# Searching the first token block's best keys in the gate stage instead of the query stage

## The chip, the core and the metric

The kernel runs on one core of one Trainium2 chip. The metric is the device time of one execution in microseconds (us); lower is better. The engines are named as the profile names them: PE is TensorE (its weight loads are PEld), DVE is VectorE, ACT is ScalarE, POOL is GpSimd, SP is SyncE, which here issues most of the DMAs. L123 is line 123 of the kernel.

## What is computed

One decoder layer over 512 tokens of width 1024. A token mixer makes a new residual stream; then a retrieval layer picks, per token and per head, 16 of 16384 experts by product keys. The part around the change is the retrieval:

```python
def chunk_fn(hc):
    q = (hc @ w_query).reshape(PEER_CHUNK, PEER_HEADS, PEER_KEY_DIM)
    s1 = jnp.einsum('chk,nk->chn', q[..., :PEER_HALF_DIM], keys_1)
    s2 = jnp.einsum('chk,nk->chn', q[..., PEER_HALF_DIM:], keys_2)
    v1, i1 = lax.top_k(s1, PEER_TOPK_HALF)
    v2, i2 = lax.top_k(s2, PEER_TOPK_HALF)
    cand = (v1[..., :, None] + v2[..., None, :]).reshape(PEER_CHUNK, PEER_HEADS, -1)
    cand_idx = (i1[..., :, None] * N_KEYS + i2[..., None, :]).reshape(PEER_CHUNK, PEER_HEADS, -1)
    top_s, pos = lax.top_k(cand, PEER_TOPK)
    experts = jnp.take_along_axis(cand_idx, pos, axis=-1)
    gate = jax.nn.softmax(top_s.astype(jnp.float32), axis=-1).astype(hc.dtype)
    u = jnp.take(expert_u, experts, axis=0)
    act = jax.nn.gelu(jnp.einsum('chkd,cd->chk', u, hc))
    v = jnp.take(expert_v, experts, axis=0)
    return jnp.einsum('chk,chkd->cd', gate * act, v)
```

There are 8 heads, 128 keys in each half, and 4 blocks of 128 tokens.

## The kernel before

The kernel is one straight program; every engine works off its own instructions in the order in which they are written. Matrices in float32 are used as the sum of two float16 parts. A *unit* is 128 x 1024 weights: `load_unit` (L112) loads it over SP's queue, `high` (L117, ACT) makes the high part, `low` (L123, DVE) the low part, four buffers each; `run_ahead` and `lows_ahead` issue these steps two to four units ahead of their use. `mm3` (L170 to L172) multiplies with three matmuls: high by high, high by low, low by high.

After the token mixer the program has these stages, told here with the names that the prediction uses.

*Query stage* (loop over `ch`, 16 *chunks*, one per head and half of the keys, and a 17th round that finishes the last). PE makes the queries of chunk `ch` for all 512 tokens, then the scores of chunk `ch - 1` against 128 keys (L744, four token blocks side by side), ACT copies them to `sc` (L746), and `top16` on DVE finds the best 16 of 128 for each of the four blocks: MAX8 (the best eight), their indices, a copy of the list with those eight struck out, MAX8 and indices again (L676 to L684). One list is 128 tokens by 128 scores; a *batch* is the lists that go through the five passes together. After chunk 8 `spend(SW)` adds pieces of the next stage's first work, `select(0, t)` for token blocks 1 to 3, from the list `fill`: generators, each `yield` naming an assumed cost in us, drawn until a budget is used up.

*Selection stage.* Token blocks 1 to 3 are selected for a dense way of computing: in each slot PE does four steps of `u_steps` (scores of all experts for these 384 tokens, a unit is eight steps and ends in an activation, L650, to `s_sb`), and DVE takes pieces of the candidates' top 16, of softmax and of decoding indices. It ends with a PE transpose of the indices of block 3 (L883) and ACT copies.

*Gate stage.* For 48 groups of 8 tokens DVE makes four one-hot tensors (`one_hots`, L907 to L910; two buffers each) from the indices and gates, one group ahead, and PE multiplies them (`w_build`, L924 and L925, 16 matmuls a group) into the matrix of gate weights, which ACT copies out (L927) and SP stores to DRAM (`wd`, L929, 1 MB for every two groups). Between the groups PE goes on with `u_steps`, 200 steps over the 48 groups, four or five a group. `spend(owed + WSP)` is called after each group, but `fill` is empty here.

*Main stage.* 128 expert tiles: PE finishes the scores of tile after tile and multiplies them, weighted by the gate matrix, with the values `vn`. Token block 0 goes a sparse way meanwhile: `block0` selects and decodes it on DVE from the lists found in the query stage, then POOL gathers its experts' rows.

The heart of the gate stage's loop, which the change does not alter except for `fill` and `WSP`:

```python
    for g in range(NG):
        nxt = one_hots(g + 1) if g + 1 < NG else None
        n = left[0] // (NG - g)
        left[0] -= n
        u_steps(n)
        w_build(g, hots)
        owed = spend(owed + WSP)
        hots = nxt
```

Of the kernel before, what the change touches and what calls it, by code (L numbers as in the profile page):

```python
# [7 lines left out]
F32 = mybir.dt.float32  # L8
# [8 lines left out]
P = 128  # L17
# [21 lines left out]
GB = 3  # L39
SW = 0.8  # L40
SWE = 15
WSP = 0.25
ADAB = 3
FU = 3
BUD = 3.6
# [19 lines left out]
def body(tc, xt, cols, c_row, ada_n, ada_t, win, pool_w, pup, cvo, wout, wq, keys, ut, un, vn, fg, out, dbg=None):  # L65
    nc = tc.nc
    V, A, G, PE, SP = nc.vector, nc.scalar, nc.gpsimd, nc.tensor, nc.sync
# [3 lines left out]
    dram = es.enter_context(tc.tile_pool(name="dram", bufs=1, space=bass.MemoryType.DRAM))  # L71
# [34 lines left out]

    x1d = dram.tile([T // P, P, D], F32, name="x1d")
    wd = dram.tile([NA // TST, P, P, TST], F32, name="wd")

    def load_unit(src, bufs=4, pool=None):  # L110
        f = (pool or stream).tile([P, 1024], F32, name="unit_f", tag="f32", bufs=bufs)
        SP.dma_start(f, src)  # L112
        return f
# [21 lines left out]
    def run_ahead(n, nl=4, nh=3, ns=2):  # L135
        for j in range(n, min(n + nl, len(units))):
            if j not in loaded:
                loaded[j] = load_unit(units[j])
        for j in range(n, min(n + nh, len(units))):
            if j not in highs:  # L140
                highs[j] = high(loaded[j], WS)
        for j in range(n, min(n + ns, len(units))):
            if j not in halves:
                halves[j] = low(loaded[j], highs[j], WS, eng=G if j in PL else None)

    def next_unit():
        n = used[0]
        used[0] += 1
        run_ahead(n)
        return halves.pop(n)  # L150

    def lows_ahead():
        run_ahead(used[0], nl=0, nh=0, ns=2)


    fill = []

    def spend(us, width=1):
        k = 0
        while us > 0 and fill:  # L160
            g = fill[k % min(width, len(fill))]
            try:
                us -= next(g)
                k += 1
            except StopIteration:
                fill.remove(g)
        return us

    def mm3(o, a, b, start, stop):
        PE.matmul(o, a[0], b[0], start=start, stop=False)  # L170
        PE.matmul(o, a[0], b[1], start=False, stop=False)  # L171
        PE.matmul(o, a[1], b[0], start=False, stop=stop)  # L172
# [343 lines left out]
    for u in range(4):  # L516
        for jj, p in enumerate(half((mxhi, mxlo))):
            j = 2 * u + jj
# [16 lines left out]
    for u in range(4):  # L535
        for jj, p in enumerate(half((ychi, yclo))):
            j = 2 * u + jj
# [81 lines left out]
    def q_tile():  # L619
        return psr.tile([P, 512], F32, name="q_ps", tag="q", bufs=2)  # L620
# [14 lines left out]
    def u_steps(n):  # L635

        while n > 0:
            if not cur:
                cur.update(i=len(S), k=0, w=next_unit(), p=ps_s.tile([P, 512], F32, name="s_ps", tag="s_ps", bufs=2)[:, 0:NA])
            k = cur["k"]  # L640
            hi, lo = cur["w"]
            s = slice(k * P, (k + 1) * P)
            mm3(cur["p"], (hi[:, s], lo[:, s]), (h2hi[:, k, NB:], h2lo[:, k, NB:]), k == 0, k == NDC - 1)
            cur["k"] += 1
            n -= 1
            if cur["k"] == UL:
                lows_ahead()
            if cur["k"] == NDC:
                sg = ring.tile([P, NA], F32, name="s_sb", tag="s_sb", bufs=NS)
                A.activation(sg, cur["p"], AF.Gelu_apprx_tanh, scale=IWS)  # L650
                S[cur["i"]] = sg
                cur.clear()
# [3 lines left out]
    for j in range(TOPK):  # L656
# [4 lines left out]
    vals, idxs = [[[(sel if t else bsel).tile([P, NH, TOPK], dt, name=f"{n}{t}{s}", tag=f"{n}{t}{s}") for s in range(2)]  # L661
                   for t in range(4)] for n, dt in (("v", F32), ("i", U32))]
# [6 lines left out]

    pieces += [(h2_piece, (hf,)) for hf in range(2)]  # L670

    def top16(ch, sc):
        hd, hf = divmod(ch, 2)
        vi = [(vals[t][hf], idxs[t][hf], wqp.tile([P, P], F32, name="s2", bufs=4)) for t in range(4)]
        for t, (v, ix, s2) in enumerate(vi):
            V.max(v[:, hd, 0:8], sc[:, t])  # L676
        for t, (v, ix, s2) in enumerate(vi):
            V.max_index(ix[:, hd, 0:8], v[:, hd, 0:8], sc[:, t])
        for t, (v, ix, s2) in enumerate(vi):
            V.match_replace(s2, v[:, hd, 0:8], sc[:, t], -3.0e38)  # L680
        for t, (v, ix, s2) in enumerate(vi):
            V.max(v[:, hd, 8:16], s2)
        for t, (v, ix, s2) in enumerate(vi):
            V.max_index(ix[:, hd, 8:16], v[:, hd, 8:16], s2)  # L684

    top = sel.tile([P, 4, NH, TOPK], F32, name="top")
    pos = sel.tile([P, 4, NH, TOPK], U32, name="pos")
# [1 line left out]
    def select(h0, t, pool=None, top=top, pos=pos):  # L689

        pool = pool or sel
        v1, v2 = [v[:, h0:h0 + 4] for v in vals[t]]
        cand = pool.tile([P, 4, NCAND], F32, name="cand", bufs=2)

        def add(a0, na, nb, o0):
            o = cand[:, :, o0:o0 + na * nb].rearrange("p h (a b) -> p h a b", b=nb)
            V.tensor_tensor(o, v1[:, :, a0:a0 + na].unsqueeze(3).to_broadcast([P, 4, na, nb]),
                            v2[:, :, None, 0:nb].to_broadcast([P, 4, na, nb]), op=OP.add)

        for a in range(5):  # L700
            add(a, 1, STAIR[a], STARTS[a])
        add(5, 3, 2, STARTS[5])
        add(8, 8, 1, STARTS[8])
        yield 0.8
        hs = range(4)
        s2 = [pool.tile([P, NCAND], F32, name="c2", bufs=8) for h in hs]
        for h in hs:
            V.max(top[:, t, h0 + h, 0:8], cand[:, h])
        yield 0.5
        for h in hs:  # L710
            V.max_index(pos[:, t, h0 + h, 0:8], top[:, t, h0 + h, 0:8], cand[:, h])
        yield 0.5
        for h in hs:
            V.match_replace(s2[h], top[:, t, h0 + h, 0:8], cand[:, h], -3.0e38)
        yield 0.5
        for h in hs:
            V.max(top[:, t, h0 + h, 8:16], s2[h])
        yield 0.5
        for h in hs:
            V.max_index(pos[:, t, h0 + h, 8:16], top[:, t, h0 + h, 8:16], s2[h])  # L720
        yield 0.5

    wqs = ExitStack()
    wqp = wqs.enter_context(tc.tile_pool(name="wqp", bufs=1, reuse_waits="tile"))
    qs = {}
    for ch in range(17):
        if ch < 16:
            if ch < 2:
                p = firsts[ch]
            else:  # L730
                hi, lo = next_unit()
                p = q_tile()
                for k in range(NDC):
                    s = slice(k * P, (k + 1) * P)
                    mm3(p, (hi[:, s], lo[:, s]), (h2hi[:, k], h2lo[:, k]), k == 0, k == NDC - 1)
                lows_ahead()
                if ch == 15:
                    run_ahead(used[0], nl=4, nh=4, ns=4)
            qs[ch] = wqp.tile([P, 512], F32, name="qs", bufs=2)
            A.activation(qs[ch], p, AF.Copy, scale=IWS)  # L740
        if ch:
            p2 = psr.tile([P, 4, P], F32, name="sc_ps", tag="sc", bufs=1)
            for t in range(4):
                PE.matmul(p2[:, t], qs[ch - 1][:, t * P:(t + 1) * P], keyt[:, (ch - 1) % 2], start=True, stop=True)  # L744
            sc = wqp.tile([P, 4, P], F32, name="sc", bufs=3)
            A.activation(sc, p2, AF.Copy)  # L746
            if ch == 16:
                u_steps(NDC)
                run_ahead(used[0], nl=4, nh=4, ns=4)
            top16(ch - 1, sc)  # L750
        if ch == 8:
            for t in range(1, 4):
                fill.append(select(0, t))
        if ch < SWE:
            spend(SW)
        if pieces:
            f, a = pieces.pop(0)
            f(*a)
# [185 lines left out]
    while fill or late:  # L944
        u_steps(4)
        slot += 1
        while late and late[0][2] + LAG <= slot:
            f, a, _ = late.pop(0)
# [3 lines left out]
    ss_.close()  # L952
    ws_ = ExitStack()
    wpool = ws_.enter_context(tc.tile_pool(name="wpool", bufs=1, side="right", reuse_waits="tile"))
    NG = NA // TG
    hots = one_hots(0)
    owed = 0.0
    left = [max(0, (NS - HOLD - len(S)) * NDC)]
# [5 lines that stand above are left out]
        w_build(g, hots)  # L964
        owed = spend(owed + WSP)
        hots = nxt
    assert not fill
    u_steps((NS - len(S)) * NDC - cur.get("k", 0))
    ws_.close()
    rs.close()  # L970
# [244 lines left out]
```

## Time and profile before

| what | us |
|---|---|
| runs, median of 3 | 1474.02 (1470.59 to 1475.1) |
| the profiled execution | 1472.85 |
| its span, first to last instruction | 1471.1 |
| PE busy in the span | 1412.7 |
| DVE busy in the span | 1270.3 |

The profile is of one execution. "Busy" is time in which an engine works on an instruction; matmuls are pipelined, so that the durations of neighbours overlap and the spacing of their starts tells more. In a row of the order of time, brackets at the end say how long the engine sat idle before it and what ended the wait. A row may join several like instructions (x4). In a row of stretches the number after PE, PEld, DVE, ACT and POOL is busy time, then come the granted TensorE clock as a share of full speed, the mean busy share of the DMA engines and GB/s. By the trace the query chunks run from 298 to 400 us, selection to 490, the gate stage to 638.

### The profile page before, as it was taken

What the parts mean: (1) busy time and instruction counts of PE and PEld (TensorE: products, weight loads), DVE (VectorE), ACT (ScalarE), POOL (GpSimd) and SP (SyncE); (2) the same over time, 40 slices, a digit from 0 to 9 for tenths busy, and PEclk for the clock granted to TensorE, in tenths of its full rate; (3) what the DMA queues carried; (4) which work ended last, traced back from release to release, by engine and by line L of the source; (5) the groups of instructions that cost most, each with busy time, mean ns of one, the idle gap of its engine ahead of it and who ended that gap; (6) DMA issues with size and microseconds to landing.
All of it is one profiled execution on the core that took longest, in us unless ns stands there. A gap on an engine that the chain in (4) does not pass through costs nothing.

```text
span 1471.1 us, 21798 instructions
## 1 busy us (share of the span) xinstructions
PE 1412.7 (96%) x7969; PEld 743.1 (51%) x7969; DVE 1270.3 (86%) x2433; ACT 669.9 (46%) x931; POOL 458.3 (31%) x427
## 2 busy tenths in 40 slices
PE   6998999999989999999999999999999999999997
PEld 2443444445545666665555555555555555444443
DVE  6899966479999999958888988888888898899877
ACT  4554374343433788854333333333333333344334
POOL 0576443200000000000454544445445445422212
PEclk9999999999999999999999999999999999999998
DMA  9554533232233477794899999999999999999953
GB/s 386 192 194 172 185 123 137 79 136 87 72 113 129 150 268 269 249 297 174 295 381 364 371 365 361 375 362 358 366 343 377 364 363 342 357 359 337 326 206 134
DMA packets 145278, 386.79 MB, mean 263 GB/s; under 512 B 10897, under 2 KB 60305, under 8 KB 141073
## 3 DMA queue, kind: packets, MB, share of 16 engines
q1 hardware_dynamic: 108304, 251.15, 48.7%
q0 software_dynamic: 36864, 134.23, 24.8%
q8 instruction: 62, 1.02, 0.3%
q14 instruction: 48, 0.39, 0.1%
HBM read 355.98 MB, written 29.36 MB: 262 GB/s over the span
## 4 chain that ended last, share of the span: by engine, by line
PE 52%; DVE 28%; DMA 7%; issue 6%; POOL 4%; ACT 4%; SPq 0%; POOLq 0%; DVEq 0%; ACTq 0%
PE acc L1093 9%; PE acc L1095 9%; PE acc L1092 9%; DVE unit_lo L123 7%; PE s_ps L172 5%; PE s_ps L170 5%; PE s_ps L171 5%; PE mm L179 4%; DMA gat<-vn,eidx 4%; DVE s_ps L327 3%; POOL gat L987 2%; DVE oh L909 2%; DVE o L907 2%; DVE ol L910 2%; DMA unit_f<-ut 1%
## 5 line engine op out<-in xcount | busy, mean ns | idle before, releaser
L123 DVE SCALAR_TENSOR_TENSOR unit_lo<-unit_f,unit_hi 128x1024 f16<-128x1024 f32 x316 | 397.0, 1266 | 83.9 <-ACT unit_hi L117 80.9
L117 ACT ACTIVATE unit_hi<-unit_f 128x1024 f16<-128x1024 f32 x316 | 330.0, 1046 | 52.9 <-DMA unit_f<-ut 40.4
L987 POOL DMA_INDIRECT gat<-un,eidx x128 | 162.5, 1270 | 586.7 <-DVE bgate L826 421.8
L172 PE MATMUL s_ps<-h2hi,unit_lo 128*128 128x384 f16 x1024 | 334.5, 327 | 7.0 <-DVE unit_lo L123 7.0
L170 PE MATMUL s_ps<-h2hi,unit_hi 128*128 128x384 f16 x1024 | 334.6, 327 | 0.0
L171 PE MATMUL s_ps<-h2lo,unit_hi 128*128 128x384 f16 x1024 | 334.5, 327 | 0.0
L1092 PE MATMUL acc<-unit_hi,ghi 128*128 128x512 f16 x768 | 291.1, 379 | 0.6 <-ACT ghi L1042 0.6
L1093 PE MATMUL acc<-unit_lo,ghi 128*128 128x512 f16 x768 | 291.1, 379 | 0.4 <-DVE unit_lo L123 0.4
L1095 PE MATMUL acc<-unit_hi,glo 128*128 128x512 f16 x768 | 229.9, 379 | 0.1
L987 POOL DMA_INDIRECT gat<-vn,eidx x128 | 158.3, 1236 | 212.0 <-DVE bacc L1011 182.0
L1042 ACT ACTIVATE ghi<-g 128x384 f16<-128x384 f32 x128 | 67.0, 523 | 293.0 <-DVE g L1038 226.8
L1011 DVE SCALAR_TENSOR_TENSOR bacc<-gat,bw,bacc 128x1024 f32<-128x1024 f32 x127 | 162.6, 1280 | 14.9 <-DMA gat<-vn,eidx 14.0
L1003 DVE SCALAR_TENSOR_TENSOR gat<-gat,h2b 128x1024 f32<-128x1024 f32 x128 | 154.4, 1221 | 21.2 <-DMA gat<-un,eidx 20.7
L650 ACT ACTIVATE s_sb<-s_ps 128x384 f32<-128x384 f32 x128 | 63.0, 492 | 222.0 <-PE s_ps L172 211.3
L172 PEld LDWEIGHTS <-unit_lo 128*128 128x128 f16 x1176 | 115.5, 98 | 95.5 <-DVE unit_lo L123 9.2
L171 PEld LDWEIGHTS <-unit_hi 128*128 128x128 f16 x1176 | 115.4, 98 | 85.8 <-issue 3.7
L170 PEld LDWEIGHTS <-unit_hi 128*128 128x128 f16 x1176 | 115.7, 98 | 84.6 <-issue 3.2
L1095 PEld LDWEIGHTS <-glo 128*128 128x128 f16 x768 | 75.0, 98 | 91.6 <-DVE glo L1045 1.5
L1092 PEld LDWEIGHTS <-ghi 128*128 128x128 f16 x768 | 75.1, 98 | 88.4 <-ACT ghi L1042 1.6
L1093 PEld LDWEIGHTS <-ghi 128*128 128x128 f16 x768 | 75.1, 98 | 86.2
L179 PEld LDWEIGHTS <-unit_hi 128*128 128x128 f16 x656 | 64.2, 99 | 91.3 <-ACT unit_hi L117 9.1
L371 POOL TENSOR_TENSOR ada_f<-ada_f,crow 128x1024 f32<-128x1024 f32 x32 | 86.0, 2705 | 69.3 <-ACT crow L482 42.9
(229 smaller groups left out, 1689.4 us busy)
## 6 DMA issues: line engine op xcount, KB each, us to landing
unit_f<-ut SPq DMA_DIRECT2D x128, 512.0 KB
unit_f<-vn SPq DMA_DIRECT2D x128, 512.0 KB
wd<-wst SPq DMA_DIRECT2D x24, 1024.0 KB
wr<-wd SPq DMA_DIRECT2D x16, 1536.0 KB
ada_f<-ada_t SPq DMA_DIRECT2D x32, 512.0 KB
unit_f<-win SPq DMA_DIRECT2D x28, 512.0 KB
unit_f<-wq SPq DMA_DIRECT2D x16, 512.0 KB
sig<-ada_n SPq DMA_DIRECT2D x4, 1024.0 KB
```

The lines of the kernel that those rows point to most:

```text
L117: A.activation(hi, f, AF.Copy, scale=scale)
L123: V.scalar_tensor_tensor(lo, f, scale, hi, op0=OP.mult, op1=OP.subtract)
L170: PE.matmul(o, a[0], b[0], start=start, stop=False)
L171: PE.matmul(o, a[0], b[1], start=False, stop=False)
L172: PE.matmul(o, a[1], b[0], start=False, stop=stop)
L179: PE.matmul(p, w[:, s], r[:, k], start=(i == 0 and k == 0), stop=(i == 2 and k == n - 1))
L987: G.indirect_dma_start(out=t, out_offset=None, in_=un if n < HK else vn, in_offset=bass.IndirectOffsetOnAxis(ap=bs["eidx"][:, k:k + 1], ax ...
L1003: V.scalar_tensor_tensor(t, t, 1.0, h2b, op0=OP.mult, op1=OP.mult, accum_out=bs["pre"][:, n:n + 1])
L1011: V.scalar_tensor_tensor(bacc, t, bw[:, k:k + 1], bacc, op0=OP.mult, op1=OP.add)
L1092: PE.matmul(acc[t][h], ghi[:, ts_], vhi[:, h * 512:(h + 1) * 512], start=st, stop=False)
L1093: PE.matmul(acc[t][h], ghi[:, ts_], vlo[:, h * 512:(h + 1) * 512], start=False, stop=False)
L1095: PE.matmul(acc[t][h], glo[:, ts_], vhi[:, h * 512:(h + 1) * 512], start=False, stop=sp)
```

## The change

Block 0's lists are no longer searched in the query stage. Its scores of each chunk, `sc[:, 0]`, are stored to a DRAM tensor `scd` over SP's queue (16 stores of 64 KB), and `top16` there works on the lists of blocks 1 to 3 only. In the gate stage a generator `block0_lists` is put in `fill`: it loads the scores back, four chunks (256 KB) at a time, two loads ahead, and runs the five passes over four lists at a time, with a `yield` after each pass. So there are 4 batches of 5 pieces, each piece four instructions. `WSP`, the budget after a group, is 0.45 instead of 0.25. What might be left over is spent after the loop.

```diff
-WSP = 0.25
+WSP = 0.45
...
+    scd = dram.tile([4, P, 4, P], F32, name="scd")
...
-    def top16(ch, sc):
-        hd, hf = divmod(ch, 2)
-        vi = [(vals[t][hf], idxs[t][hf], wqp.tile([P, P], F32, name="s2", bufs=4)) for t in range(4)]
-        for t, (v, ix, s2) in enumerate(vi):
-            V.max(v[:, hd, 0:8], sc[:, t])
...
+    def top16(lists, pool, bufs):
+
+        vi = [(vals[t][ch % 2][:, ch // 2], idxs[t][ch % 2][:, ch // 2], sc,
+               pool.tile([P, P], F32, name="s2", bufs=bufs)) for t, ch, sc in lists]
+        for v, ix, sc, s2 in vi:
+            V.max(v[:, 0:8], sc)
+        yield 0.9
+        for v, ix, sc, s2 in vi:
+            V.max_index(ix[:, 0:8], v[:, 0:8], sc)
+        yield 1.1
+        for v, ix, sc, s2 in vi:
+            V.match_replace(s2, v[:, 0:8], sc, -3.0e38)
+        yield 1.1
+        for v, ix, sc, s2 in vi:
+            V.max(v[:, 8:16], s2)
+        yield 0.9
+        for v, ix, sc, s2 in vi:
+            V.max_index(ix[:, 8:16], v[:, 8:16], s2)
+        yield 1.1
+
+    def block0_lists(pool):
+        scs = []
+        for c in range(2):
+            scs.append(pool.tile([P, 4, P], F32, name="sc0", bufs=2))
+            SP.dma_start(scs[c], scd[c])
+        for c in range(4):
+            yield from top16([(0, 4 * c + j, scs[c][:, j]) for j in range(4)], pool, 4)
+            if c < 2:
+                scs.append(pool.tile([P, 4, P], F32, name="sc0", bufs=2))
+                SP.dma_start(scs[c + 2], scd[c + 2])
...
-            top16(ch - 1, sc)
+            SP.dma_start(scd[(ch - 1) // 4][:, (ch - 1) % 4], sc[:, 0])
+            for _ in top16([(t, ch - 1, sc[:, t]) for t in range(1, 4)], wqp, 3):
+                pass
...
+    fill.append(block0_lists(wpool))
     NG = NA // TG
...
-    assert not fill
+    spend(1e9)
```

The lines below the new code move by 1 to 21: the low part is L124, the one-hots are L927 to L930, the passes L678 to L690.

DVE at the start of the gate stage, before the change (`o` and `oh`, `ol` are the four one-hots of a group):

```order
L907 TENSOR_TENSOR o_4518<-aT,i_2447 128x1024
L908 TENSOR_TENSOR o_4517<-aT,i_2447 128x1024
L909 TENSOR_TENSOR oh<-o_4518,gT 128x1024
L910 TENSOR_TENSOR ol<-o_4518,gT 128x1024
L907 TENSOR_TENSOR o_4564<-aT,i_2447 128x1024
L908 TENSOR_TENSOR o_4563<-aT,i_2447 128x1024
L909 TENSOR_TENSOR oh<-o_4564,gT 128x1024
L910 TENSOR_TENSOR ol<-o_4564,gT 128x1024
L123 SCALAR_TENSOR_TENSOR unit_lo<-unit_f,unit_hi 128x1024
```

The same place in the changed kernel (`sc_4484` holds the scores of the first four chunks, `v` the values found):

```order
L678 MAX v_2450<-sc_4484 128x8
L678 MAX v_2451<-sc_4484 128x8
L678 MAX v_2450<-sc_4484 128x8
L678 MAX v_2451<-sc_4484 128x8
L927 TENSOR_TENSOR o_4497<-aT,i_2448 128x1024
L928 TENSOR_TENSOR o_4496<-aT,i_2448 128x1024
L929 TENSOR_TENSOR oh<-o_4497,gT 128x1024
L930 TENSOR_TENSOR ol<-o_4497,gT 128x1024
L124 SCALAR_TENSOR_TENSOR unit_lo<-unit_f,unit_hi 128x1024
L927 TENSOR_TENSOR o_4542<-aT,i_2448 128x1024
L928 TENSOR_TENSOR o_4541<-aT,i_2448 128x1024
```

A piece of four stands ahead of the third group's one-hots, and so on, one piece for every two or three groups; the last piece (L690, of the fourth batch) stands ahead of the one-hots of the 45th group.

SP's queue where the gate stage begins, in the changed kernel (`ut` are the units of the expert scores; in brackets the semaphores that an entry waits for):

```order
L113 DMA unit_f<-ut 128x1024 [waits DMAHW7_49,DVE_49]
L697 DMA sc_4484<-scd 128x512 [waits PE_49]
L697 DMA sc_4486<-scd 128x512
L949 DMA wd<-wst 128x2048 [waits Activation_49]
L113 DMA unit_f<-ut 128x1024 [waits DMAHW0_49,DVE_49]
L949 DMA wd<-wst 128x2048 [waits Activation_49]
```

Before, the 24th load of `ut` is followed by the first store of `wd`; now the two first loads of scores stand between them, and the first of them waits for PE.

## Rows read from the trace of the kernel before

**Rows 1.** The page: busy time of the engines, share of the span, instructions.

```profile
PE 1412.7 (96%) x7969; PEld 743.1 (51%) x7969; DVE 1270.3 (86%) x2433; ACT 669.9 (46%) x931; POOL 458.3 (31%) x427
```

**Rows 2.** Stretches: length, busy time of each engine, granted clock, DMA share, GB/s.

```profile
426.00:430.00 4.00, 4.00 (x15) 1.96 (x14) 3.96 (x31) 0.00 (x0) 0.00 (x0) 0.57 0.40 131
430.00:490.00 60.00, 58.24 (x361) 34.50 (x359) 59.45 (x196) 26.88 (x43) 0.00 (x0) 1.00 0.39 123
490.00:600.00 110.00, 107.49 (x1033) 75.33 (x1032) 110.00 (x168) 93.11 (x109) 0.00 (x0) 1.00 0.72 247
600.00:640.00 40.00, 37.86 (x346) 26.33 (x345) 34.34 (x51) 31.88 (x39) 0.00 (x0) 1.00 0.72 244
640.00:1265.00 625.00, 624.60 (x3383) 330.84 (x3382) 537.01 (x785) 237.58 (x327) 276.77 (x217) 1.00 0.95 347
```

**Rows 3.** DVE in order of time, query stage: start, length, instruction, count.

```profile
350.20 0.87 DVE L676 MAX8 v<-sc 128x8 f32<-128x128 f32 x4 [0.17 <-ACT sc L746]
...
354.89 1.20 DVE L123 SCALAR_TENSOR_TENSOR unit_lo<-unit_f,unit_hi 128x1024 f16<-128x1024 f32 x1
...
369.74 0.87 DVE L676 MAX8 v<-sc 128x8 f32<-128x128 f32 x4
...
376.71 0.87 DVE L676 MAX8 v<-sc 128x8 f32<-128x128 f32 x4
```

**Rows 4.** PE in order of time, query and selection stages.

```profile
354.55 1.05 PE L744 MATMUL sc_ps<-keyt,qs 128*128 128x128 f32 x8
...
360.62 1.05 PE L744 MATMUL sc_ps<-keyt,qs 128*128 128x128 f32 x8
...
425.88 0.40 PE L172 MATMUL s_ps<-h2hi,unit_lo 128*128 128x384 f16 x1 [4.89 <-DVE unit_lo L123]
```

**Rows 5.** PE's waits from 290 to 495: total, times, longest.

```profile
PE s_ps L172 <- DVE unit_lo L123: 7.0, 5, 4.9
```

**Rows 6.** DVE in order of time, end of the query stage.

```profile
403.94 3.49 DVE L123 SCALAR_TENSOR_TENSOR unit_lo<-unit_f,unit_hi 128x1024 f16<-128x1024 f32 x3
407.35 0.86 DVE L676 MAX8 v<-sc 128x8 f32<-128x128 f32 x4
...
417.84 0.53 DVE L708 MAX8 top<-cand 128x8 f32<-128x50 f32 x4
```

**Rows 7.** ACT in order of time, end of the query stage.

```profile
392.06 0.60 ACT L746 ACTIVATE sc<-sc_ps 128x512 f32<-128x512 f32 x1 [0.23 <-PE sc_ps L744]
...
404.59 1.05 ACT L117 ACTIVATE unit_hi<-unit_f 128x1024 f16<-128x1024 f32 x1
```

**Rows 8.** DVE in order of time, gate stage.

```profile
489.99 0.68 DVE L907 TENSOR_TENSOR o<-aT,i 128x1024 f16<-128x1024 f16 x1
...
509.13 1.21 DVE L123 SCALAR_TENSOR_TENSOR unit_lo<-unit_f,unit_hi 128x1024 f16<-128x1024 f32 x1
...
515.08 1.21 DVE L123 SCALAR_TENSOR_TENSOR unit_lo<-unit_f,unit_hi 128x1024 f16<-128x1024 f32 x1
...
632.70 0.69 DVE L910 TENSOR_TENSOR ol<-o,gT 128x1024 f16<-128x1024 f16 x1
```

**Rows 9.** ACT's evictions of finished score units, 395 to 500: durations, first and last start.

```profile
L650 ACT ACTIVATE s_sb<-s_ps x21: 471/490/491, 404.2 to 495.5; 128x384 f32<-128x384 f32 x21
```

**Rows 10.** PE in order of time, gate stage.

```profile
515.60 0.22 PE L924 MATMUL w_ps<-o,oh 128*128 128x128 f16 x1
...
516.50 0.33 PE L170 MATMUL s_ps<-h2hi,unit_hi 128*128 128x384 f16 x1
...
518.45 0.22 PE L924 MATMUL w_ps<-o,oh 128*128 128x128 f16 x1
...
637.75 0.22 PE L925 MATMUL w_ps<-o,ol 128*128 128x128 f16 x1
```

**Rows 11.** Waits from 490 to 640: total, times, longest.

```profile
ACT unit_hi L117 <- DMA unit_f<-ut: 17.9, 15, 3.5
PEld L925 <- DVE ol L910: 6.8, 19, 0.5
```

More of the change, by code (lines that the diff above doesn't have):

```diff
@@ L670, in body @@
     pieces += [(h2_piece, (hf,)) for hf in range(2)]
-    def top16(ch, sc):
-        hd, hf = divmod(ch, 2)
-        vi = [(vals[t][hf], idxs[t][hf], wqp.tile([P, P], F32, name="s2", bufs=4)) for t in range(4)]
-        for t, (v, ix, s2) in enumerate(vi):
-            V.max(v[:, hd, 0:8], sc[:, t])
[L677 to L684, printed above, removed]
+    def top16(lists, pool, bufs):
[26 more added lines that the diff above has]
+                SP.dma_start(scs[c + 2], scd[c + 2])
     top = sel.tile([P, 4, NH, TOPK], F32, name="top")
```

## The prediction

> **What bounds the kernel now.** I read the busy line first [rows 1]: PE (TensorE) is busy 96% of the span and DVE (VectorE) 86%. That is an average, so next I cut the span into stretches [rows 2]. Over 640 to 1265 us PE is busy 624.60 of 625 us: whatever delays the start of that stretch delays the end by as much, and nothing there gives it back. From 490 to 600 us, the stage that builds the gate matrix, DVE is busy 110.00 of 110 us; in the selection stage before it, 59.45 of 60. The change takes work from DVE in the query stage and gives it to DVE in the gate stage, so three questions decide: which engine is late at the end of the query stage, who paces the gate stage, and how many microseconds move.
>
> **What moves.** One batch of the key search (four lists of 128 scores, five passes) runs from 350.20, its first MAX8, to 354.89, where the next instruction starts [rows 3]: 4.69 us, or 1.17 us a list. Block 0 has 16 lists (8 heads, 2 halves), so 16 x 1.17 = **18.8 us** of DVE time leave the query stage. They come back in the gate stage in the same instructions and shapes, as 20 pieces of four. I take 18.8 on both sides.
>
> **Query and selection stages: 7.5 us gained.** A chunk takes PE 6.07 us from score matmul to score matmul [rows 4]. Up to chunk 8 DVE needs 4.69 plus 1.13 for a low part (a third of the 3.41 us from 403.94 to 407.35 [rows 6]), 5.82 in all, and keeps up, so those eight lists give nothing back. From then on a piece of the first selection joins in, the batches come 6.97 us apart [rows 3], and DVE falls behind. PE feels that once in earnest: from 420.99 it sits idle 4.89 us for a low part, until 425.88 [rows 4], and then runs four microseconds at a granted clock of 0.57 [rows 2], most of it at 1.2 instead of 2.4 GHz, worth 4 x (1 - 0.57) = 1.7 us. All five waits of this kind come to 7.0 us [rows 5].
>
> With three lists a batch is 3.52 us, so from chunk 8 DVE needs some 6.97 - 1.17 = 5.8 us a chunk, under 6.07, and no backlog forms. I follow DVE through the last chunks. The scores of chunk 13 are there at 392.06 + 0.60 = 392.7 [rows 7]. Then come a batch (3.5), a piece of selection (6.97 - 4.69 - 1.13, some 1.2) and three low parts (3.4): 400.8. Another batch: 404.3. The next low part needs the high part that ACT starts at 404.59 and that takes 1.05 [rows 7], so DVE waits 1.4 us, until 405.7; then 1.13 and the last batch end at **410.3**, where the kernel before starts selection at 417.84 [rows 6]. DVE is the later engine in the selection stage, so the first one-hots start at 489.99 - 7.5 = 482.5 instead of 489.99 [rows 8]. PE alone could be there sooner: 19 more units of scores after the eviction of the first at 404.2 [rows 9], 8 steps of 0.49 us each [rows 10], end near 479. Bounds of this gain: 5.0 if only the large stall goes; 8.7 if PE loses neither the 7.0 us of waits nor the 1.7 of slow clock.
>
> **Gate stage: 18.8 us lost.** Two groups of the gate stage take DVE 5.95 us, low part to low part, 509.13 to 515.08 [rows 8]. PE needs 2.85 us for one group, 515.60 to 518.45 [rows 10], so 5.70 for two; the other 0.25 us it waits, mostly for the one-hot `ol` (19 waits, 6.8 us [rows 11]). DVE paces the stage, by a small margin, and has no gap to put a piece in. The first one-hots start at 489.99 and the last end at 632.70 + 0.69 = 633.4 [rows 8], 143.4 us of DVE; with the pieces 143.4 + 18.8 = 162.2. The order of the changed kernel puts the last piece ahead of the 45th of 48 one-hot groups, so all of it counts. From 482.5 the last one-hots then end at 644.7.
>
> **End of the gate stage: 3.0 us gained.** Before, PE ends 637.75 + 0.22 = 638.0 [rows 10], 4.6 us after DVE, for the last eight groups carry five score steps instead of four (200 steps over 48 groups), which makes PE the slower one: 0.90 + 5 x 0.49 = 3.33 us a group against DVE's 2.41 (four one-hots, from 489.99 on at 0.60) + 5/8 x 1.13 = 3.11. With the pieces DVE is the slower one until the 44th group, so only three groups can pile up a lag: 0.9 for the last group's matmuls and 3 x 0.22, about 1.6 us. PE ends at 644.7 + 1.6 = 646.3, 8.3 us later than 638.0. Bounds: no gain (ACT, which waits 17.9 us for unit loads in this stage [rows 11], delays PE at the end as before), or all 4.6.
>
> **The copies: nothing, with an upper bound.** Sixteen stores of 64 KB are queued on SP among the unit loads; each waits for ACT's copy of the scores, and the next load waits behind it. The loads run three units ahead of their use, some 18 us at 6.07 a chunk, so I cost this at nothing; with that cover gone, the late high part at the end of the query stage could slip as far again as DVE already waits for it, 1.4 us. In the gate stage the first load of scores stands in SP's queue behind the 24th unit load and waits for PE, by my reading for the last transposes of the selection stage, near 481.6. The first MAX wants it after two groups of one-hots, at 482.5 + 4.8 = 487.3, which leaves more than 5 us. If it is late, DVE stops with all one-hots behind it, and PE with it; the longest wait for a load of twice the size in this stage is 3.5 us [rows 11]. So 0 to 3.5, and I take 0, for the queue has little else at that moment. The second load goes with the first, and the other two stand ten groups ahead of their use.
>
> **Sum.** -7.5 + 18.8 - 3.0 = **+8.3 us**. The profiled execution took 1472.85 us (span 1471.1 and 1.75 around it): 1481.1, so **1481 us**. The median of the runs shown, 1474.02, is 1.2 higher than the profiled execution; 8.3 on it gives 1482.3, within the range. All good ends together: 18.8 - 8.7 - 4.6 = +5.5, 1478.4; all bad ones: 18.8 - 5.0 + 3.5 + 1.4 = +18.7, 1491.6.
>
> **A rule on the clock.** In the changed gate stage PE idles up to 1 us ahead of nearly every second group, 23 us in all. The rows: the clock stays 1.00 over 490 to 600 with 19 short waits, and is 0.57 right after the one idle stretch of 4.89 us [rows 2, 4, 11]. I keep the full clock.
> The Trainium skill ("TensorE: Matmul & The Clock Gate", "A second HAM failure mode: psum-queue depth-cycling") warns that an engine which idles briefly and often between groups of matmuls can swing between its two clock levels. By the rows the sum stays +8.3, by that rule it is larger; the trace does not bear the rule out so far, but its waits are shorter than those to come.
>
> **The rivals.**
> *Same* (about 1476). In the last third of the gate stage (600 to 640: DVE 34.34 of 40, PE 37.86 [rows 2]) ACT waits for unit loads and PE for ACT, and a piece there might cost nothing. With the five or so pieces after 600 free (5 us) and both gains at their good ends: 18.8 - 8.7 - 4.6 - 5 = +0.5; halfway from there to the +5.5 is +3. Against it: DVE has no idle time until its one-hots are nearly done.
> *Faster* (1465). PE could be the true pace of the gate stage, DVE's one-hots being stretched by their two-deep buffers without a wait showing. Twenty pieces over some 22 pairs of groups are 0.85 us a pair, which has eight one-hot instructions; if each could run 0.11 us quicker than its 0.60, the pieces are free and the 7.5 us are what is left: 1472.85 - 7.5 = 1465.4. That is the point from which it decides. Against it: PE waits for `ol`, not DVE for PE.
> *Much slower* (1486 and up). The first MAX waits 3.5 us for its scores, PE with it, and the clock halves once more (1.7): 8.3 + 5.2 = +13.5, 1486; with bad ends elsewhere 1490.
> *Slow clock* (1591). If PE ran at 1.2 GHz through the whole stage, a pair would take it 11.4 us instead of DVE's 6.8: 24 x 4.6 = 110 us more. This is the end of what the rule above would do.
>
> **How the numbers follow.** Forecast 0.70, same 0.15, faster 0.07, much slower 0.06, slow clock 0.02. The range 1474 to 1489 leaves out the faster case, part of the same case, the slow clock and the tail of the much slower one. A measurement of this kernel tells about 0.3% (4.4 us) from no change, so slower begins at 1478.4: the forecast's low end lies on that line, and I count 0.06 of the forecast to the same side. Slower 0.72, same 0.21, faster 0.07.
>
> **What would show it.** Right: PE without the long idle stretch near 421; the first one-hots near 482.5; DVE without a gap from there to about 645; PE's waits for the one-hots in the gate stage up from 6.8 us to some 23; granted clock 1.00 there; PE gapless from then on and shifted by some 8 us. Wrong: a first MAX that waits long for a load; one-hots that come closer together; a granted clock well under 1 in the gate stage; selection that starts no earlier.

## The result, and the profile after

The change costs time: the median of 5 runs is 1483.28 us (1480.89 to 1484.91), beside 1475.1 for the kernel before in the same comparison. The ratio is **1.0061**, 95% interval 1.0044 to 1.0077. The forecast was 1481, slower.

The profiled execution after took 1484.91 us (span 1483.1), 12.1 more than that of before. Of these, 3.6 us arise ahead of the query stage, in code that the change does not touch: the first score matmul starts at 315.1 instead of 311.5, and in the profiles of the experiments at 312.5 to 315.0. The new DRAM tensor does not show as the cause: in query_only and query_last8, which lack it, that matmul starts at 313.4 and 314.4. So I set the two side by side from that matmul on. These are the rows by line that give the positions (durations min/median/max in ns; then the first and the last start), before:

```profile
L744 PE MATMUL sc_ps<-keyt,qs x128: 272/275/377, 311.5 to 400.0; 128*128 128x128 f32 x128
L910 DVE TENSOR_TENSOR ol<-o,gT x48: 678/682/687, 491.8 to 632.7; 128x1024 f16<-128x1024 f16 x48
L925 PE MATMUL w_ps<-o,ol x384: 217/219/230, 492.5 to 637.8; 128*128 128x128 f16 x192
L1092 PE MATMUL acc<-unit_hi,ghi x768: 377/379/389, 661.2 to 1460.4; 128*128 128x512 f16 x192
```

and after, with the first one-hots (`o`) in addition:

```profile
L762 PE MATMUL sc_ps<-keyt,qs x128: 272/275/377, 315.1 to 404.8; 128*128 128x128 f32 x128
L927 DVE TENSOR_TENSOR o<-aT,i x48: 662/677/686, 487.3 to 646.4; 128x1024 f16<-128x1024 f16 x48
L930 DVE TENSOR_TENSOR ol<-o,gT x48: 672/681/686, 489.1 to 648.2; 128x1024 f16<-128x1024 f16 x48
L945 PE MATMUL w_ps<-o,ol x384: 217/219/230, 489.8 to 650.2; 128*128 128x128 f16 x192
L1113 PE MATMUL acc<-unit_hi,ghi x768: 377/379/390, 673.7 to 1473.2; 128*128 128x512 f16 x192
```

Less the first score matmul, in us, with the experiments that come below (before's first one-hots: 489.99 [rows 8] - 311.55). Each row is one profiled execution. The differences here and in the text are rounded after the subtraction, so that they can be 0.1 off those of the rows as printed:

| | last score matmul | first one-hots | last `ol` | last gate matmul | first `acc` matmul | last `acc` matmul |
|---|---|---|---|---|---|---|
| before | 88.4 | 178.4 | 321.2 | 326.2 | 349.7 | 1148.8 |
| after | 89.7 | 172.2 | 333.1 | 335.1 | 358.6 | 1158.0 |
| copies_only | 89.5 | 178.5 | 320.7 | 325.3 | 348.7 | 1147.9 |
| gate_only | 89.4 | 178.4 | 339.3 | 341.4 | 364.9 | 1163.9 |
| query_only | 88.4 | 170.9 | 313.4 | 318.3 | 341.8 | 1142.3 |
| query_last8 | 88.4 | 170.9 | 313.7 | 318.7 | 342.2 | 1142.8 |
| late_store | 88.4 | 170.9 | 331.9 | 333.9 | 357.4 | 1157.1 |
| post_gate | 89.9 | 174.1 | 316.2 | 321.2 | 350.0 | 1151.0 |
| post_gate_pool | 88.4 | 170.9 | 313.2 | 317.0 | 341.7 | 1139.2 |
| post_gate_last8 | 88.4 | 170.9 | 313.2 | 317.5 | 341.0 | 1139.0 |

Read the first two rows from left to right. The score matmuls end 1.3 later, the gate stage starts 6.3 earlier, its one-hots spread over 160.9 instead of 142.7 us (+18.2), PE's lag behind the last `ol`, start to start, shrinks from 5.1 to 2.0 (-3.0), and the 8.9 us with which the main stage starts late are still there at its end (9.2).

The busy line of the page says little of this (DVE's share stays 86%):

```profile
PE 1417.8 (96%) x7969; PEld 743.5 (50%) x7969; DVE 1272.3 (86%) x2433; ACT 673.0 (45%) x931; POOL 463.4 (31%) x427
```

The stretches say more (length, busy time of PE, PEld, DVE, ACT and POOL, granted clock, DMA share, GB/s):

```profile
421.00:426.00 5.00, 5.00 (x33) 3.04 (x31) 4.96 (x42) 2.59 (x4) 0.00 (x0) 1.00 0.34 104
487.00:650.00 163.00, 148.51 (x1360) 99.50 (x1359) 163.00 (x347) 125.75 (x146) 0.00 (x0) 1.00 0.67 228
650.00:1275.00 625.00, 624.50 (x3392) 331.29 (x3389) 535.79 (x785) 238.38 (x329) 281.21 (x216) 1.00 0.95 347
```

Where PE stood still for 4.89 us before and then ran at 0.57 [rows 2, 4], it is busy throughout, at full clock. In the gate stage DVE has no gap in 163 us, and PE is idle for 14.5 of them. In the main stage PE is as gapless as before. The waits of the gate stage, 487 to 650 (total, times, longest):

```profile
PEld L945 <- DVE ol L930: 15.7, 33, 0.5
PEld L944 <- DVE oh L929: 12.9, 25, 1.2
PE w_ps L945 <- DVE ol L930: 10.0, 29, 0.4
PE w_ps L944 <- DVE oh L929: 4.3, 8, 0.8
```

The weight loader's waits for the one-hots were 8.0 us (6.8 for `ol` [rows 11], 1.2 for the first `oh`) and are 28.6 now, for `oh` and `ol`. Those of PE itself were 1.2 and are 14.3. DVE where the first piece stands (start, length):

```profile
491.51 0.68 DVE L930 TENSOR_TENSOR ol<-o,gT 128x1024 f16<-128x1024 f16 x1
492.11 0.87 DVE L678 MAX8 v<-sc 128x8 f32<-128x128 f32 x4
492.89 0.67 DVE L927 TENSOR_TENSOR o<-aT,i 128x1024 f16<-128x1024 f16 x1
```

The MAX8 has no bracket, so it waited for nothing: its scores, asked for at 482.3, took 4.2 us and were there 5.6 us ahead. It stands between two groups of one-hots and takes 0.78 us of DVE, start to start.

### The profile page after: what moved, and what is told of

The parts are those of the page before. It is cut to its first block, busy times and chain, and to the rows that moved or that the text cites. A ratio compares the mean times of both kernels' runs of the same rounds, so it can differ in the third digit from the quotient of the medians.

```text
span 1483.1 us, 21833 instructions
## 1 busy us (share of the span) xinstructions
PE 1417.8 (96%) x7969; PEld 743.5 (50%) x7969; DVE 1272.3 (86%) x2433; ACT 673.0 (45%) x931; POOL 463.4 (31%) x427
## 4 chain that ended last, share of the span: by engine, by line
PE 51%; DVE 17%; DMA 2%; issue 1%; ACT 1%; ACTq 0%; DVEq 0%; SPq 0%
PE acc L1114 10%; PE acc L1113 10%; PE acc L1116 10%; PE s_ps L173 7%; PE s_ps L171 7%; PE s_ps L172 7%; DVE unit_lo L124 4%; DVE oh L929 2%; DVE ol L930 2%; DVE o L927 2%; DVE o L928 1%; DMA unit_f<-ut 1%; DMA wr<-wd 1%; ACT unit_hi L118 0%; DVE eq L879 0%
## 5 line engine op out<-in xcount | busy, mean ns | idle before, releaser
L124 DVE SCALAR_TENSOR_TENSOR unit_lo<-unit_f,unit_hi 128x1024 f16<-128x1024 f32 x316 | 397.6, 1270 | 77.0 <-ACT unit_hi L118 75.8
L173 PE MATMUL s_ps<-h2hi,unit_lo 128*128 128x384 f16 x1024 | 333.9, 326 | 1.5 <-DVE unit_lo L124 1.5
L1008 POOL DMA_INDIRECT gat<-vn,eidx x128 | 163.7, 1279 | 205.7 <-DVE bacc L1032 181.3
L1032 DVE SCALAR_TENSOR_TENSOR bacc<-gat,bw,bacc 128x1024 f32<-128x1024 f32 x127 | 162.5, 1280 | 18.1 <-DMA gat<-vn,eidx 17.4
## 6 DMA issues: line engine op xcount, KB each, us to landing
wr<-wd SPq DMA_DIRECT2D x16, 1536.0 KB, 15.1
```

The lines of the kernel that those rows point to most:

```text
L124: V.scalar_tensor_tensor(lo, f, scale, hi, op0=OP.mult, op1=OP.subtract)
L1008: G.indirect_dma_start(out=t, out_offset=None, in_=un if n < HK else vn, in_offset=bass.IndirectOffsetOnAxis(ap=bs["eidx"][:, k:k + 1], ax ...
L1032: V.scalar_tensor_tensor(bacc, t, bw[:, k:k + 1], bacc, op0=OP.mult, op1=OP.add)
```

## The experiments

Theory: DVE paces the gate stage, so the search costs its full DVE time there; the query stage gives back about 7.5; the copies cost nothing. Rivals: the copies hold up SP's queue; the gate stage has slack; the search could be free at another place. The first three kernels do one part of the change alone; the others ask where the rest of the gain went and where the pieces would cost nothing. Diffs are against the changed kernel.

**copies_only**: scores are stored and loaded, but all four lists are searched in the query stage.

```diff
-            yield from top16([(0, 4 * c + j, scs[c][:, j]) for j in range(4)], pool, 4)
+            yield 5.1
...
-            for _ in top16([(t, ch - 1, sc[:, t]) for t in range(1, 4)], wqp, 3):
+            for _ in top16([(t, ch - 1, sc[:, t]) for t in range(4)], wqp, 4):
```

> All four blocks' lists are searched in the query stage as before; the 16 stores of scores and the four loads of the gate stage are there as in the changed kernel, with none of the search behind them. My theory (only DVE's time in the gate stage counts, the copies are hidden): 0 us against before, within 2, and the first one-hots no later than before, counted from the first score matmul of the query stage. Rival (the copies hold up SP's queue and with it the unit loads): 3 us or more later, with ACT's waits for unit loads longer than before in the query or the gate stage. If the changed kernel's slower part before its query stage (3.7 us in its profiled execution) comes from the new DRAM tensor, it shows here too.

Measured: 1472.66 us, ratio 0.9988 [0.9977, 1.0]. The score matmuls end 1.1 later, yet the first one-hots start at 178.5, as before: DVE is the later engine in the selection stage and hides it. So the copies, placed as the change places them, cost PE a microsecond even where no search moves, and cost the kernel nothing only as long as DVE is late.

**gate_only**: the query stage searches all four lists, and the gate stage searches block 0 once more.

```diff
-            for _ in top16([(t, ch - 1, sc[:, t]) for t in range(1, 4)], wqp, 3):
+            for _ in top16([(t, ch - 1, sc[:, t]) for t in range(4)], wqp, 4):
```

> All four blocks' lists are searched in the query stage as before, and block 0's once more in the gate stage as in the changed kernel: what the change adds, alone. My theory: the 18.8 us of DVE come on the path less 3 us of lag at the end of the gate stage: 15 to 17 us later than before, near 1491, one-hots from first to last start some 161 us instead of 143. Rival (part of the pieces is hidden behind PE, and the changed kernel lost its time elsewhere): 8 us later or less.

Measured: 1487.76 us, ratio 1.0092 [1.0079, 1.0105]. The one-hots spread over 160.8 us (+18.1), the main stage starts 15.2 later, so the lag at the end gives back 2.9. That is the second half of the sum with no gain ahead of it. The medians differ by 13.3 us, less than the 15 to 17 expected; the positions, up to the last `acc` matmul (+15.1), agree with them.

**query_only**: block 0 is not searched at all (its lists hold constants, so its part of the main stage works on other data), nothing is stored, and the gate stage has no pieces.

```diff
...
+    for s in range(2):
+        for j in range(TOPK):
+            G.memset(vals[0][s][:, :, j], -0.01 * j)
+            G.memset(idxs[0][s][:, :, j], 7 * j + s)
...
-            SP.dma_start(scd[(ch - 1) // 4][:, (ch - 1) % 4], sc[:, 0])
...
-    fill.append(block0_lists(wpool))
```

> Block 0's lists are searched nowhere (its values and indices are filled with constants by POOL), and no scores are stored or loaded: what the change removes, alone. My theory: the gate stage starts some 6.5 us sooner than before, keeps its 143.4 us of DVE and its lag of PE at the end, and the kernel ends 6 to 7.5 us sooner, near 1468. Rival (the query stage is paced by PE, and what DVE saves there is hidden): less than 2 us sooner.

Measured: 1468.95 us, ratio 0.9972 [0.9957, 0.9986]. The gate stage starts 7.5 earlier. With the copies it was 6.3, so the copies take 1.2 of the gain. The medians differ by 5.5 us, somewhat less than the 6 to 7.5 expected: the main stage starts 7.9 earlier, but takes 800.5 us from its first to its last `acc` matmul, 1.3 more than before.

**late_store**: the whole change, but each store enters SP's queue one chunk later.

```diff
+    held = None
...
-            SP.dma_start(scd[(ch - 1) // 4][:, (ch - 1) % 4], sc[:, 0])
+            for c, s in [held] * (held is not None) + [(ch - 1, sc)] * (ch == 16):
+                SP.dma_start(scd[c // 4][:, c % 4], s[:, 0])
+            held = ch - 1, sc
```

> The changed kernel, but each store of scores stands one chunk later in SP's queue, so that no unit load waits behind a store that waits for ACT. My theory (in chunk 15 a unit load and its high part are asked for together, the load stood behind the store of chunk 13, and ACT held the last scores back by 1.3 us): the last score matmul comes 88.5 us after the first instead of 89.7, the gate stage starts 1.3 us sooner, and the kernel ends 1 to 1.5 us before the changed kernel. Rival (the stores' own traffic is what delays): no difference.

Measured: 1481.21 us, ratio 1.0052 [1.0039, 1.0065]. The gate stage starts at 170.9, as in query_only, and the main stage moves the same 1.2 with it. The medians do not settle this: each beside the kernel before in its own comparison, the changed kernel is 8.2 us slower and this one 7.8, and their intervals overlap. The place shows in the rows. In the changed kernel SP issues the store of a chunk's scores and, only behind it, the next two loads of expert units:

```profile
396.25 0.32 SPq L768 DMA_DIRECT2D scd<-sc  x1
396.66 0.86 SPq L113 DMA_DIRECT2D unit_f<-ut  x2
```

ACT stands at such a load, and the copies of the last chunks' scores are queued behind it:

```profile
400.58 1.06 ACT L118 ACTIVATE unit_hi<-unit_f 128x1024 f16<-128x1024 f32 x1 [3.41 <-DMA unit_f<-ut]
401.86 1.06 ACT L118 ACTIVATE unit_hi<-unit_f 128x1024 f16<-128x1024 f32 x1 [0.22 <-DMA unit_f<-ut]
```

so PE waits 2.28 us for an eviction of scores:

```profile
403.94 1.16 PE L762 MATMUL sc_ps<-keyt,qs 128*128 128x128 f32 x8 [2.28 <-ACT sc L764]
```

With the late store that wait is 1.01 again, what it was before:

```profile
400.27 1.16 PE L763 MATMUL sc_ps<-keyt,qs 128*128 128x128 f32 x8 [1.01 <-ACT sc L765]
```

Since DVE paces what follows, the delay counts where DVE meets it: at the last low part of the query stage, whose high part ACT makes after the delayed copies. DVE's wait for it, in the changed kernel and then with the late store:

```profile
410.50 1.23 DVE L124 SCALAR_TENSOR_TENSOR unit_lo<-unit_f,unit_hi 128x1024 f16<-128x1024 f32 x1 [2.32 <-ACT unit_hi L118]
```

```profile
406.83 1.23 DVE L124 SCALAR_TENSOR_TENSOR unit_lo<-unit_f,unit_hi 128x1024 f16<-128x1024 f32 x1 [1.06 <-ACT unit_hi L118]
```

**query_last8**: as query_only, but the first eight chunks keep their search; only chunks 9 to 16 (`ch` 8 to 15 in the expectation, which counts from 0) lose block 0's.

```diff
...
-            for _ in top16([(t, ch - 1, sc[:, t]) for t in range(1, 4)], wqp, 3):
+            for _ in top16([(t, ch - 1, sc[:, t]) for t in range(1 if ch > 8 else 0, 4)], wqp, 4):
```

> Block 0's lists of chunks 8 to 15 are searched nowhere, those of chunks 0 to 7 in the query stage as before; no copies, no pieces in the gate stage. My theory (the first eight chunks are paced by PE and give nothing back): the same gain as with all 16 lists left out, the gate stage 7 to 7.6 us sooner than before, counted from the first score matmul, and the end 5 to 7 us sooner. Rival (the gain grows with the DVE time taken out): half, 3 to 4 us.

Measured: 1469.29 us, ratio 0.9972 [0.9962, 0.9982]; the first one-hots at 170.9, as without all sixteen. The first eight lists give nothing back: DVE keeps up there. The medians alone would not have said so: they differ by 4.2 us, below the 5 to 7 expected and next to the rival's 3 to 4. Here too the main stage is longer, 800.6 us, and constants stand in half of block 0's lists.

**post_gate**: the pieces stand behind the last one-hots, beside the remaining score steps, with all four loads of scores issued ahead.

```diff
...
-    fill.append(block0_lists(wpool))
+    lists0 = block0_lists(wpool)
+    next(lists0)
...
+    fill.append(lists0)
+    spend(5.0)
+    n = (NS - len(S)) * NDC - cur.get("k", 0)
+    while n > 0:
+        u_steps(min(n, 2))
+        n -= 2
+        spend(0.9)
     spend(1e9)
-    u_steps((NS - len(S)) * NDC - cur.get("k", 0))
```

> As the changed kernel, but the pieces stand behind the loop of the gate stage, among the last four units of scores before the main stage; all four loads of scores are issued at the start of the gate stage. My theory: DVE waits there for loads of units (its busy time was 31.99 of 50 us from 640 to 690), so 18.8 us of pieces fit nearly whole beside PE, and the 6 to 7 us saved in the query stage are kept: 1467 to 1470. Rival (low parts of units and the first tiles of the main stage come late behind the pieces, and PE stalls): at or above the time before.

Measured: 1474.5 us, ratio 0.9998 [0.9988, 1.0007]. My number for it missed. The gate stage is short again, but two things eat the gain. The first one-hots start 3.1 later than in query_only. PE's wait for the scores is 2.47 us here, until 401.51, and the stretch behind it runs at a lower granted clock:

```profile
404.00:409.00 5.00, 5.00 (x25) 2.73 (x24) 1.56 (x10) 1.36 (x3) 0.00 (x0) 0.77 0.94 313
```

So the next expert scores come late (ACT waits 3.63 us for the first, in query_only 1.95), and behind them the high part that DVE's last low part wants: DVE waits 4.20 us for it, in query_only 1.05.

And between the last gate matmul and the first `acc` matmul lie 28.8 us, 23.5 in query_only. The waits from 628 to 680:

```profile
PE acc L1117 <- ACT ghi L1067: 4.7, 1, 4.7
DVE g L1063 <- DMA wr<-wd: 4.1, 1, 4.1
```

PE waits for the high part of a gate, ACT for DVE, DVE for the first load of `wr`, and SP issues that one only at 652.14:

```profile
652.14 3.98 SPq L1056 DMA_DIRECT2D wr<-wd  x2
```

The queue's own waits in the same stretch name what it stood for:

```profile
SPq L1056 <- DVE s L684: 11.3, 1, 11.3
```

L684 strikes out the eight best of a list and is the last pass that reads the scores loaded back; of the fourth batch it ends at 652.08. My reading is that the first buffer of `wr` lies in memory which the pieces' scores hold until then; the next run tests it.

**post_gate_pool**: post_gate with the late store, and the pieces' buffers in a pool of their own, opened ahead of the one-hots' pool.

```diff
...
+    p0s = ExitStack()
+    p0 = p0s.enter_context(tc.tile_pool(name="p0", bufs=1, side="right", reuse_waits="tile"))
...
+    lists0 = block0_lists(p0)
...
```

> As the run with the pieces behind the gate stage, but the scores and the struck lists of the pieces lie in a pool of their own that the main stage's first loads don't overwrite, and the stores stand one chunk later. My theory (there the first load of the gate matrix waited until DVE had done with the pieces' buffers, and the late store took 1.3 us more): the first load of the gate matrix is issued some 8 us after the gate stage as before, PE has no wait of 4.7 us at the start of the main stage, and of the 7.6 us saved in the query stage 5 to 7 are kept: near 1468. Rival (DVE's low parts and first tiles themselves come late behind 18.8 us of pieces): the wait at the start of the main stage stays at 3 us or more, and the time is that of before.

Measured: **1465.65 us**, ratio 0.9946 [0.9933, 0.9958]: faster than both kernels. The first load of `wr` is issued at 637.1, with no such wait of its own, PE's wait for the gate is down to 0.6, and PE has hardly a gap where the pieces stand:

```profile
PE acc L1123 <- ACT ghi L1073: 0.6, 1, 0.6
```

```profile
620.00:660.00 40.00, 39.04 (x265) 23.56 (x263) 37.97 (x152) 21.73 (x28) 0.00 (x0) 1.00 0.95 311
```

Of the two edits, the store acts ahead of the gate stage (first one-hots at 170.9, in post_gate 174.1), the pool behind it (last gate matmul to first `acc` 24.6 us, in post_gate 28.8). The main stage starts at 341.7, where query_only, without any search of block 0, has 341.8: here the search is free. The 7.8 us by which the median beats before's are more than the 5 to 7 expected.

**post_gate_last8**: the same with the lists of chunks 9 to 16 alone moved.

```diff
...
-            for _ in top16([(t, ch - 1, sc[:, t]) for t in range(1, 4)], wqp, 3):
+            for _ in top16([(t, ch - 1, sc[:, t]) for t in range(1 if ch > 8 else 0, 4)], wqp, 4):
```

> As the run before, with only the lists of chunks 8 to 15 moved: 9.4 us of pieces behind the gate stage instead of 18.8, and eight stores. My theory: the same gain in the query stage, and still less in DVE's way at the start of the main stage: 6 to 7.5 us sooner than before, near 1467. Rival: if the gain grows with the DVE time taken out, 3 to 4 us.

Measured: 1466.19 us, ratio 0.9947 [0.9935, 0.9959]. With half of the lists moved the time is the same within the interval.

## Why the prediction was right

- **Who paces the gate stage: right.** 18.8 forecast, +18.2 in the change, +18.1 alone (gate_only). DVE is gapless over the stage. PE's weight loads wait 28.6 us for one-hots and PE itself 14.3, where I said 23. The rival that PE sets the pace (faster) would have kept the one-hots' spread at 142.7, and falls; so does "same", which wanted some 5 us of the pieces free: 18.2 of 18.8 counted.
- **PE's lag at the end of the gate stage: right.** -3.0 forecast, -3.0 measured; gate_only gives -2.9 with no gain ahead of the stage. (In the working, 0.90 + 5 x 0.49 is 3.35 and not 3.33, which leaves the lag at about 1.6.)
- **The gain in the query and selection stages: mechanism and size right, net too large.** 7.5 forecast; query_only, where nothing is stored, and late_store both measure 7.5. With three lists the batches come 6.07 us apart, PE's pace, and DVE waits for the scores of 13 of the 16 chunks, so no backlog forms. DVE's wait for the late high part, 1.4 in the forecast, is 1.06 in late_store. Also right: the stall near 421 is gone, and the first eight lists give nothing. The change itself got 6.3.
- **The copies at nothing: the step that failed.** "The loads run three units ahead of their use" was true of most chunks, and not of the last: there two units are asked for together, and both loads stand behind a store that itself waits for ACT. I had named 1.4 as the upper bound, at the late high part that DVE waits for, and there it came out: the wait is 2.32 us instead of 1.06, and the gate stage starts 1.2 later. The way to it I had not seen: a late load holds up ACT, ACT the last scores, and PE waits 2.28 instead of 1.01. copies_only shows why a test of the copies alone would have missed it: while DVE was late, nobody waited for that microsecond.
- **The first load of scores: cost right, its wait misread.** Issued at 482.3 (I said near 481.6), with over 5 us to spare. But it cannot have waited for the selection's last transposes, since PE does one at 486.10. In SP's order of time it follows the unit load ahead of it at once:

```profile
481.92 0.33 SPq L113 DMA_DIRECT2D unit_f<-ut  x1
482.30 0.98 SPq L697 DMA_DIRECT2D sc<-scd  x2
```

- **Sum.** -6.3 + 18.2 - 3.0 = 8.9, the last gate matmul's shift (335.12 - 326.21); +8.3 was forecast. The medians of the runs differ by 8.2. That this is so near to 8.3 is in part luck: the interval reaches from 6.5 to 11.4 us, and two errors partly offset each other, the copies (+1.2) and the pieces (18.2 instead of 18.8). Of the 2.3 us between 1481 and the median, most is the start of the sum: 1472.85, where the median before is 1475.1.
- **The clock.** The granted clock is 1.00 over 487 to 650, the higher of its two levels, though PE waited 37 times for one-hots, 0.8 us at the longest, and was idle for 14.5 us in all. The rule of the Trainium skill ("TensorE: Matmul & The Clock Gate", "A second HAM failure mode: psum-queue depth-cycling"), that an engine which idles briefly and often between groups of matmuls can swing between its clock levels, is not borne out by these waits; the slow-clock rival falls.
- **Left open.** From the first to the last `acc` matmul the profiles take 797.5 to 800.9 us, in code that is the same in all (block 0's data are not, in query_only and query_last8). So the 1.6 us by which post_gate_pool is better behind the gate stage (from 341.7 to 1139.2 it takes 797.5, before 799.2) are not explained.

## What to carry to other kernels

Moving work to another stage gains only if its engine does not pace that stage: here the same 18.8 us of VectorE cost 18.2 in the gate stage and nothing in the stretch right behind it. The place decides about memory too: at the good place the pieces still cost 5.3 us (28.8 against 23.5) while their buffers held memory that the next stage's first load wanted. And a store in a queue that also carries loads is priced by what it waits for: put it behind the loads that the next instructions want.

## What the runs showed of the hardware

Two waits of nearly the same length at the same place left different clocks. Behind a wait of 2.47 us (post_gate) the granted clock fell, to 0.50, the lower of its two levels, over 403 to 406 and 0.77 over 404 to 409; behind one of 2.28 us (the changed kernel) PE kept 1.00 over the same 5 us:

```profile
404.00:409.00 5.00, 5.00 (x34) 3.37 (x35) 4.18 (x25) 1.88 (x2) 0.00 (x0) 1.00 0.71 211
```

What separates the two was not tried. And the code ahead of the query stage, which the change leaves alone, reached the first score matmul 3.6 us apart in two executions, which is why positions were compared from there.
